# Moving the short heads' attention steps later against the projection, in a hybrid decoder layer on one core

## The chip, the core and the metric

The kernel runs on one core of one Trainium2 chip. The metric is the device time of one execution in microseconds. A core has five engines with queues of their own: TensorE (PE, matrix products), VectorE (DVE), ScalarE (ACT), GpSimd (POOL) and SyncE (SP, which issues transfers). PE writes only to PSUM, and DVE and ACT fetch its results from there.

## The reference, cut to what matters

One layer on x of 1024 positions by 2048 features, in float32:

```python
hn = rmsnorm(h, norm_mix_g)
sb_q, sb_k, sb_v, sb_g, df_q, df_k, df_v, df_g = split(hn @ w_in)
# stick-breaking heads (8 of 128): w[t,s] = beta[t,s] * prod_{s<j<t} (1 - beta[t,j]), s < t
# differential heads (8 of 2 x 64): (softmax1 - lam * softmax2) @ v, then a norm of each head's row
mixed = concat([sb_out * silu(sb_g), df_out * silu(df_g)])
h = h + mixed @ w_out
gate = sigmoid(rmsnorm(h, norm_ple_g) @ w_ple_gate)
h = h + gate * (p @ w_ple_proj)
return rmsnorm(h, norm_final_g)
```

The product of (1 - beta) over the positions between is computed as a running product along the row (a scan on VectorE).

## The kernel before, in words

**Precision.** Every large product is made of three matmuls: both operands are split into a high part in float32r and a low part (the rest), and high x high, high x low and low x high are accumulated. So each tile that becomes an operand costs a copy on ACT (high) and a subtraction on DVE (low): whi L149 and wlo L150 for weights, awh L375 and awl L376 for attention weights, v L345 and L346, q and k L1020 and L1021.

**Stages.** From 0 to about 375 us the values and gates of the short heads are projected for all positions. Then come two halves of 512 positions each, half 1 first and half 0 ("the second half") after it. In each half a loop (from L985) goes over the heads 8 to 15, the differential ones, and then 0 to 7, the stick-breaking ones ("short heads"). A differential head has two units of projection (q and k, then v and gate), a short head has one (q and k), and loads its v and gate by `load_vg` (L994). From about 1740 us the out-projection runs, then the gate, the embedding's projection and the last norm.

**Units and ticks.** `unit` (L205) makes two 128 x 512 results from 16 blocks of features: 32 times three matmuls of 512 columns (L219 to L221). After each three it calls `side.tick()`. One such step is a tick. The out-projection's first 64 products tick too (L1224 on), and what is left is run at once behind them.

**What sets the order.** `Side` (L186 to L200) keeps a queue of (due tick, step), sorted by the tick, with steps of one tick in the order in which they were added. PE's order is fixed by the order in which these steps are emitted (a manual schedule for TensorE). For ACT, DVE, POOL and SP a scheduler orders the instructions by its own reckoning; `turn` of a short head raises the priority of its splits. Each engine works its queue in order.

**The steps of a head** (`attention`, L268, returns them with due ticks counted from the end of the head's unit):
- *weights(rb, c)*, for the four row blocks of 128 queries: scores on PE (L289 to L297), mask on DVE (L302, L304), for a short head two sigmoids on ACT (pt L318, bt L319), scan (L320) and product (L321) on DVE. Differential heads: maximum, two exponentials and their combination (L325 to L336), for two components c.
- *values*: v is transposed into PSUM (vps, L343) and split into v (L345 on ACT, L346 on DVE). In half 1 it is also stored for the second half.
- *turn(pr, g)*: two row blocks form a pair pr. The pair's weights against two key blocks are transposed on PE (tp, L359) and split by `parts`: the first turn of a pair gives a triangular `lead` (L368, L369), the rest awh (L375, ACT) and awl (L376, DVE).
- *mix(pr, g)*: av += v x weights on PE (L391 with lead, L394, L395 and L396). Behind the last mix av is fetched (sm: L401 on ACT, L402 on DVE) and multiplied into sg, the head's gate (L405). With pair 1 done, `mixed` sends the result into sums in DRAM: the tensor comb_d, by a plain transfer on SP and accumulating transfers on POOL.
- *norm(pr)*, differential heads only: sums of squares on PE (L422, L423), an inverse root in `rstd_from` (L88 to L95, on ACT and DVE).

tp, vps, av and the norm's sums share two PSUM buffers (tag "t"). In half 0 a head has four turns in pair 0 and three in pair 1, and all keys; in half 1 two and one.

**The due ticks before** (L429 to L455). A short head has its row blocks at b, b + 3, b + 7 and b + 11, values at b + 14, pair 0's turns from b + 16 every 4 ticks (GAPS), pair 1's from 16 (half 0) or 12 (half 1) ticks later (SECOND), each mix one gap behind its turn; the last mix of pair 1 comes 2 later. b is 6, for head 0 it is 12. The last differential head, hd 15, is `tight`: its row blocks and turns are closer together than those of the others.

**At the end of a unit** q and k are taken from acc (qk L1018, then L1020, L1021), v and the gate are scaled (vf L1046, gf L1047), and sg is made with a sigmoid on ACT (L1050) and a product on DVE (L1055). In half 0 the other half's keys and values (k2, v2) are loaded by POOL (L1064, L1068), and the head's steps are put into the queue.

Of the kernel before, what the change touches and what calls it, by code (L numbers as in the profile page):

```python
# [14 lines left out]
F32R = mybir.dt.float32r  # L15
# [5 lines left out]
P = 128  # L21
# [12 lines left out]

GAPS, GAPD = 4, 6
SECOND = 16, 12
PRIO = 300
LATD = 11, 20
NORM_LAT = 11
# [4 lines left out]
def build(nc, tc, ap):  # L44
    with ExitStack() as ctx:
        _body(ctx, nc, tc, ap)


def _body(ctx, nc, tc, ap):
# [7 lines left out]
    V, G, A, T = nc.vector, nc.gpsimd, nc.scalar, nc.tensor  # L57
# [180 lines left out]
    v_d = dram.tile([2 * H, P, 2 * HALF], F32R, name="v_d", tag="v_d")  # L238
# [29 lines left out]
    def attention(at, pz, half, hd, q, qz, K, KL, VV, sg, vf):  # L268

        sb = hd < H  # L270
# [68 lines left out]
        def values():  # L339

            vps = pp.tile([P, 4, P], F32, name="vps", tag="t")
            for j in range(4):
                T.transpose(vps[:, j, :], vf[:, j * P:(j + 1) * P], ident)  # L343
            v = at.tile([P, 2, 4, P], F32R, name="v", tag="v")
            A.copy(v[:, 0], vps)  # L345
            V.tensor_tensor(v[:, 1], vps, v[:, 0].bitcast(F32), op=ALU.subtract)  # L346
            if half == 1:
                G.dma_start(v_d[hd], v.rearrange("p a b c -> p (a b c)"))
            VV.insert(0, v)

        def turn(pr, g):

# [8 lines left out]
            wl = at.tile([P, 2, 2 * P], F32R, name="awl", tag="awl")  # L361
            with tc.high_priority(offset=PRIO if sb else 0):
                parts(pr, g, tp, wh, wl)

        def parts(pr, g, tp, wh, wl):
            if g == 0:
                lead = at.tile([P, 2, P], F32R, name="lead", tag="lead")
                A.copy(lead[:, 0], tp[:, 0, 0:P])  # L368
                V.tensor_tensor(lead[:, 1], tp[:, 0, 0:P], lead[:, 0].bitcast(F32), op=ALU.subtract)  # L369
                wjs[pr, g] = [lead, (wh[:, 1, :], wl[:, 1, :])]  # L370
                o = slice(1, 2)
            else:
                wjs[pr, g] = [(wh[:, j, :], wl[:, j, :]) for j in range(2)]
                o = slice(0, 2)
            A.copy(wh[:, o, :], tp[:, o, :])  # L375
            V.tensor_tensor(wl[:, o, :], tp[:, o, :], wh[:, o, :].bitcast(F32), op=ALU.subtract)  # L376
# [54 lines left out]
        n1 = n0 - 1  # L431
        gap = GAPS if sb else GAPD
        if sb:
            b = 12 if hd == 0 else 6
            ss, t0 = [[b], [b + 3], [b + 7], [b + 11]], b + 16
            t1 = t0 + SECOND[half]
        else:
            tight = hd == 2 * H - 1
            s0, s1, s2, t0 = ([0, 1], [3, 5], [7, 9], 16) if tight else ([0, 2], [5, 8], [12, 15], 19)
            gap = 4 if tight else gap  # L440
            last = t0 + gap * (n0 - 1)
            s3 = [last + 1, last + (3 if tight else 5)]
            ss = [s0, s1, s2, s3]
            t1 = s3[-1] + (13 if tight else LATD[half])
        steps = [(t, partial(weights, rb, c)) for rb, ts in enumerate(ss) for c, t in enumerate(ts)]
        steps.append((t0 - 2 if sb else ss[1][-1] + 2, values))
        for pr, t, n in ((0, t0, n0), (1, t1, n1)):
            for g in range(n):
                if g:
                    steps.append((t + gap * g, partial(mix, pr, g - 1)))  # L450
                steps.append((t + gap * g, partial(turn, pr, g)))
            steps.append((t + gap * n + (2 if sb and pr else 0), partial(mix, pr, n - 1)))
            if not sb:
                steps.append((t + gap * n + (7 if tight else NORM_LAT), partial(norm, pr)))
        return steps  # L455

    with tc.tile_pool(name="at", bufs=2) as at, tc.tile_pool(name="pz", bufs=2, space=PSUM) as pz:
# [20 lines left out]
        def ftile():  # L478
            return ev.tile([P, HALF], F32, name="hc", tag="f", bufs=4)
# [256 lines left out]
        for u in range(0, H, 2):  # L736
            aa = [pp.tile([P, HALF], F32, name="pa", tag="acc", bufs=2) for _ in range(2)]
            for i in range(2):
                gv.product(u + i, 0, "A11", aa[i], True)
                s1 = ftile()  # L740
# [139 lines left out]
        for ph in range(2):  # L880
            for u in range(H):
                last = ph == 1 and u == H - 1
# [5 lines left out]
                s1 = s1s.pop(u) if early else ev.tile([P, HALF], F32, name="s1", tag="sq", bufs=2)  # L888
                if ph:
                    a = pp.tile([P, HALF], F32, name="pa", tag="acc", bufs=2)  # L890
# [6 lines left out]
                if ph == 0 and u % 3 == 2:  # L897
                    b, c = [pp.tile([P, HALF], F32, name="pb", tag="acc", bufs=2) for _ in range(2)]
                else:
                    bc = pz.tile([P, 2, HALF], F32, name="pbc", tag="z")  # L900
                    b, c = bc[:, 0, :], bc[:, 1, :]
# [66 lines left out]
        for half in (1, 0):  # L968
# [15 lines left out]
            for hd in (ORDER0, ORDER1)[half]:  # L984
                sb = hd < H  # L985
# [71 lines left out]
                VV = []  # L1057
                if half == 1:
                    G.dma_start(k_d[hd].rearrange("p (a b) -> p a b", a=2), k[:, :, 0:HALF])
                    if not sb:  # L1060
                        G.dma_start(kl_d[hd - H], KL[:, 0, :])
                else:
                    k2 = at.tile([P, 2, HALF], F32R, name="k2", tag="k2")
                    G.dma_start(k2.rearrange("p a b -> p (a b)"), k_d[hd])  # L1064
                    if not sb:
                        G.dma_start(KL[:, 1, :], kl_d[hd - H])
                    v2 = at.tile([P, 2, 4, P], F32R, name="v2", tag="v2")
                    G.dma_start(v2.rearrange("p a b c -> p (a b c)"), v_d[hd])  # L1068
                    K.append(k2)
                    VV.append(v2)  # L1070
                side.add(attention(at, pz, half, hd, q, qz, K, KL, VV, sg, vf))
                if hd >= H:
                    for kt in (2 * (hd - H), 2 * (hd - H) + 1):
# [12 lines left out]
        def pair(nm, tag, dt=F32, shape=(P, 2, HALF)):  # L1086
            return at.tile(list(shape), dt, name=nm, tag=tag, bufs=BUFS.get(tag, 2))
# [142 lines left out]
        for u in range(0, 8, 2):  # L1230
            aa = [pp.tile([P, HALF], F32, name="pa", tag="acc", bufs=2) for _ in range(2)]
            for i in range(2):
                product(u + i, 0, "A11", aa[i], True, tick=True)
                s1 = ftile()
# [66 lines left out]
        for ph in range(2):  # L1301
            for u in range(8):
                last = ph == 1 and u == 7
# [7 lines left out]
                s1 = s1s.pop(u) if early else ev.tile([P, HALF], F32, name="s1", tag="sq", bufs=2)  # L1311
                if ph:
                    a = pp.tile([P, HALF], F32, name="pa", tag="acc", bufs=2)
# [6 lines left out]
                if ph == 0 and u % 3 == 2:  # L1320
                    b, c = [pp.tile([P, HALF], F32, name="pb", tag="acc", bufs=2) for _ in range(2)]
                else:
                    bc = pz.tile([P, 2, HALF], F32, name="pbc", tag="z")
                    b, c = bc[:, 0, :], bc[:, 1, :]
# [63 lines left out]
        s2 = SumSq(ev, "ssq")  # L1388
# [54 lines left out]
        for u in range(8):  # L1443
# [9 lines left out]
            if u == 0:  # L1453
# [5 lines left out]
                s2 = SumSq(ev, "ssq")  # L1459
# [7 lines left out]
        for pc in range(4):  # L1467
            raw = wp.tile([P, 2, 2, 2, P], F32, name="wraw", tag="wraw", bufs=2)
            nc.sync.dma_start(raw, ap["w_gate"][7][pc])
            for k2 in range(2):  # L1470
# [3 lines left out]
                else:  # L1474
                    t = pair(f"wz{kk}", H1[kk], F32R, (P, 2, 2, 2, P))
# [5 lines left out]
        for tq in range(2):  # L1481
            ts = slice(tq * Q, tq * Q + Q)
            acc = [pp.tile([P, Q], F32, name=f"acq{c}", tag="acc", bufs=2) for c in range(2)]
            for c in range(2):
                for kk in range(8):
                    for kh in range(2):
                        xh, xl = X[kk + 8 * kh]
                        first = kk == 0 and kh == 0
                        last = kk == 7 and kh == 1
# [5 lines left out]
            for c in range(2):  # L1495
                t = h[0, 7 + 8 * c][:, ts]
# [73 lines left out]
```

## Time and profile before

| | us |
|---|---|
| median of 3 runs | 2514.29 (2512.94 to 2517.38) |
| the profiled execution | 2515.73 |
| its span in the trace | 2514.0 |
| PE, DVE, ACT, POOL busy | 2421.5, 1792.6, 1215.5, 279.6 |
| mean granted clock of PE | 0.991 of full speed |
| projection of short heads' v and gate | 0 to 375 |
| half 1: differential heads, short heads | 385 to 735, 735 to 1010 |
| half 0: differential heads, short heads | 1010 to 1480, 1480 to 1740 |
| out-projection and the rest | 1740 to 2514 |

Times in the profile count from the span's start. A line of a group names source line, engine, operation, output <- input, how often, then busy time, the mean duration of one, and the idle time ahead of it with its releaser. PE's matmuls are pipelined: one of 512 columns is shown as 0.39 us long, while the next starts after 0.227. So idle time between shown ends is less than what is lost against the usual distance of starts; where the text says "by starts", it counts that distance. In the timeline, [1.09 <-DVE awl L376] means that PE stood still for 1.09 us and that awl released it.

### The profile page before, as it was taken

What the parts mean: (1) busy time and instruction counts of PE and PEld (TensorE: products, weight loads), DVE (VectorE), ACT (ScalarE), POOL (GpSimd) and SP (SyncE); (2) the same over time, 40 slices, a digit from 0 to 9 for tenths busy, and PEclk for the clock granted to TensorE, in tenths of its full rate; (3) what the DMA queues carried; (4) which work ended last, traced back from release to release, by engine and by line L of the source; (5) the groups of instructions that cost most, each with busy time, mean ns of one, the idle gap of its engine ahead of it and who ended that gap; (6) DMA issues with size and microseconds to landing.
All of it is one profiled execution on the core that took longest, in us unless ns stands there. A gap on an engine that the chain in (4) does not pass through costs nothing.

```text
span 2514.0 us, 31908 instructions
## 1 busy us (share of the span) xinstructions
PE 2421.5 (96%) x11434; PEld 2005.8 (80%) x11434; DVE 1792.6 (71%) x3010; ACT 1215.5 (48%) x2067; POOL 279.6 (11%) x361
## 2 busy tenths in 40 slices
PE   8999999999999999999999988998899999999997
PEld 6787878888888887888888877887787887787886
DVE  6888777777777768688888876778577674546554
ACT  5233345555555445555566654445423224546433
POOL 1211110000000001000000000110111112330110
PEclk9999999999999999999999999999999999999998
DMA  8777654544354556343434344546746777343333
GB/s 292 255 263 223 214 193 143 164 130 151 122 153 145 168 176 186 107 113 106 122 114 122 110 122 97 143 124 186 232 162 213 169 189 230 110 137 104 131 109 101
DMA packets 167472, 397.72 MB, mean 158 GB/s; under 512 B 18897, under 2 KB 23249, under 8 KB 167313
## 3 DMA queue, kind: packets, MB, share of 16 engines
q1 hardware_dynamic: 131040, 302.07, 37.6%
q0 software_dynamic: 36272, 93.60, 14.4%
q8 instruction: 90, 1.47, 0.2%
q14 instruction: 70, 0.57, 0.1%
HBM read 297.03 MB, written 106.95 MB: 161 GB/s over the span
## 4 chain that ended last, share of the span: by engine, by line
PE 79%; DVE 10%; DMA 5%; ACT 4%; issue 3%; SPq 0%; DVEq 0%; POOL 0%; ACTq 0%
PE acc L219 16%; PE acc L220 16%; PE acc L221 16%; PE pbc L518 4%; PE pbc L516 4%; PE pbc L517 4%; PE tp L359 2%; DVE st L320 2%; PE pa L518 1%; PE pa L516 1%; PE pa L517 1%; PE av L396 1%; PE z L297 1%; PE z L298 1%; PE av L395 1%
## 5 line engine op out<-in xcount | busy, mean ns | idle before, releaser
L219 PE MATMUL acc<-xh,whi 128*128 128x512 f32 x1568 | 629.3, 401 | 1.5 <-DVE gt L1183 1.5
L221 PE MATMUL acc<-xh,wlo 128*128 128x512 f32 x1568 | 613.9, 392 | 0.0
L220 PE MATMUL acc<-xl,whi 128*128 128x512 f32 x1568 | 613.8, 391 | 0.0
L150 DVE TENSOR_TENSOR wlo<-wraw,whi 128x1024 fp32r<-128x1024 f32 x252 | 312.6, 1240 | 243.0 <-ACT whi L149 236.5
L149 ACT CAST whi<-wraw 128x1024 fp32r<-128x1024 f32 x252 | 264.9, 1051 | 295.5 <-PE acc L220 264.3
L221 PEld LDWEIGHTS acc<-xh,wlo 128*128 128x128 f32 x1568 | 295.5, 188 | 64.8
L219 PEld LDWEIGHTS acc<-xh,whi 128*128 128x128 f32 x1568 | 296.0, 189 | 57.2 <-issue 2.4
L220 PEld LDWEIGHTS acc<-xl,whi 128*128 128x128 f32 x1568 | 296.5, 189 | 54.7 <-issue 0.5
L606 ACT CAST wpr<-T 128x512 fp32r<-128x512 f32 x128 | 78.0, 621 | 317.4 <-DVE T L564 313.1
L375 ACT CAST awh<-tp 128x256 fp32r<-128x256 f32 (+1 forms) x160 | 80.1, 501 | 150.2 <-PE tp L359 124.8
L376 DVE TENSOR_TENSOR awl<-tp,awh 128x256 fp32r<-128x256 f32 (+1 forms) x160 | 92.8, 580 | 65.3 <-ACT awh L375 63.7
L328 ACT ACTIVATE et<-z,mx 128x512 f32<-128x512 f32 (+7 forms) x128 | 94.5, 738 | 51.1 <-DVE mx L325 49.5
L111 POOL TENSOR_TENSOR ssq<-ssq,sq 128x512 f32<-128x512 f32 x56 | 83.6, 1494 | 304.8 <-ACT sq L110 254.1
L320 DVE TENSOR_TENSOR_SCAN st<-pt 128x511 f32<-128x511 f32 (+3 forms) x64 | 86.5, 1352 | 23.8 <-ACT pt L318 23.8
L325 DVE TENSOR_REDUCE mx<-z 128x1 f32<-128x512 f32 (+7 forms) x128 | 96.4, 753 | 1.2
L620 DVE TENSOR_TENSOR wpr<-T,wpr 128x512 fp32r<-128x512 f32 x128 | 87.7, 685 | 5.8 <-ACT wpr L606 3.9
L396 PE MATMUL av<-awl,v 128*128 128x256 f32 x256 | 76.1, 297 | 16.0 <-DVE awl L376 15.9
L516 PE MATMUL pbc<-cS,wpr 128*128 128x512 f32 x224 | 87.4, 390 | 3.2 <-DVE u L1327 1.6
L517 PE MATMUL pbc<-cS,wpr 128*128 128x512 f32 x224 | 87.2, 389 | 0.0
L518 PE MATMUL pbc<-cS,wpr 128*128 128x512 f32 x224 | 87.2, 389 | 0.0
L318 ACT ACTIVATE pt<-z 128x512 f32<-128x512 f32 (+3 forms) x64 | 41.6, 651 | 81.6 <-DVE z L304 80.4
L394 PE MATMUL av<-awh,v 128*128 128x256 f32 x256 | 72.8, 284 | 5.5 <-ACT awh L375 5.5
(399 smaller groups left out, 5354.2 us busy)
## 6 DMA issues: line engine op xcount, KB each, us to landing
wraw<-w_in SPq DMA_DIRECT2D x192, 512.0 KB, 3.6
wraw<-w_gate SPq DMA_DIRECT2D x64, 512.0 KB, 3.6
wraw<-w_out SPq DMA_DIRECT2D x72, 256.0 KB, 3.6
wraw<-w_vg SPq DMA_DIRECT2D x71, 256.0 KB, 4.2
comb_d<-sg POOLq DMA_DIRECT2D x48, 256.0 KB, 7.5
spare<-xT SPq DMA_DIRECT2D x44, 256.0 KB, 4.2
xl<-h_d SPq DMA_DIRECT2D x40, 256.0 KB, 4.3
vghalf_d<-hc POOLq DMA_DIRECT2D x32, 256.0 KB, 4.1
```

Source lines behind the costliest of these rows:

```text
L149: A.copy(hi[:, o], raw[:, o])
L150: V.tensor_tensor(lo[:, o], raw[:, o], hi[:, o].bitcast(F32), op=ALU.subtract)
L219: T.matmul(acc[c], hi[:, k2, kh, c, :], xh, start=first, stop=False)
L220: T.matmul(acc[c], hi[:, k2, kh, c, :], xl, start=False, stop=False)
L221: T.matmul(acc[c], lo[:, k2, kh, c, :], xh, start=False, stop=last)
L320: V.tensor_tensor_scan(st[:, off + 1:nkey], pt[:, off:nkey - 1], pt[:, off:nkey - 1], initial=1.0, op0=ALU.mult, op1=ALU.bypass)
L325: V.reduce_max(mx, z[:, vw], axis=AX.X, negate=True)
L328: A.activation(et[:, vw], z[:, vw], AF.Exp, bias=mx[:, 0:1], accum_out=l)
L396: T.matmul(av, vv[:, 0, blk % 4, :], wl, start=False, stop=last)
L516: T.matmul(o, wh[:, w], xh, start=start and k == 0, stop=False, skip_group_check=True)
L517: T.matmul(o, wh[:, w], xl, start=False, stop=False, skip_group_check=True)
L518: T.matmul(o, wl[:, w], xh, start=False, stop=k == 3, skip_group_check=True)
```

## The change

- Short heads start their steps later: `LAG` gives b = 13 for all in half 1, and in half 0 b = 20 for head 0, 19 for head 1, down to 13 for head 7. So in half 0 a head's steps follow the previous head's after 31 ticks, while units follow after 32.
- In pair 1 of a short head, turns come every 5 ticks instead of 4, with each mix 5 behind its turn. The last mix comes at 15 ticks after the pair's start (14 before).
- Head 15's row blocks go from [0,1], [3,5], [7,9] to [0,2], [4,7], [10,13], its pair 0 starts at 18 (16), turns come every 5 ticks (4), the last row block at +1 and +5 (+1 and +3) behind the last turn, and pair 1 starts 14 (13) behind that.
- v2 is allocated and loaded in `values` instead of at the unit's end, and the list of v tiles is filled in order.

No computation is added or left out.

```diff
+LAG = 20, 13
...
             V.tensor_tensor(v[:, 1], vps, v[:, 0].bitcast(F32), op=ALU.subtract)
+            VV.append(v)
             if half == 1:
                 G.dma_start(v_d[hd], v.rearrange("p a b c -> p (a b c)"))
-            VV.insert(0, v)
+            else:
+                v2 = at.tile([P, 2, 4, P], F32R, name="v2", tag="v2")
+                G.dma_start(v2.rearrange("p a b c -> p (a b c)"), v_d[hd])
+                VV.append(v2)
...
         if sb:
-            b = 12 if hd == 0 else 6
+            b = LAG[half] - hd * (1 - half)
             ss, t0 = [[b], [b + 3], [b + 7], [b + 11]], b + 16
             t1 = t0 + SECOND[half]
         else:
             tight = hd == 2 * H - 1
-            s0, s1, s2, t0 = ([0, 1], [3, 5], [7, 9], 16) if tight else ([0, 2], [5, 8], [12, 15], 19)
-            gap = 4 if tight else gap
+            s0, s1, s2, t0 = ([0, 2], [4, 7], [10, 13], 18) if tight else ([0, 2], [5, 8], [12, 15], 19)
+            gap = 5 if tight else gap
             last = t0 + gap * (n0 - 1)
-            s3 = [last + 1, last + (3 if tight else 5)]
+            s3 = [last + 1, last + 5]
             ss = [s0, s1, s2, s3]
-            t1 = s3[-1] + (13 if tight else LATD[half])
+            t1 = s3[-1] + (14 if tight else LATD[half])
...
         for pr, t, n in ((0, t0, n0), (1, t1, n1)):
+            d = gap + 1 if sb and pr else gap
             for g in range(n):
                 if g:
-                    steps.append((t + gap * g, partial(mix, pr, g - 1)))
-                steps.append((t + gap * g, partial(turn, pr, g)))
-            steps.append((t + gap * n + (2 if sb and pr else 0), partial(mix, pr, n - 1)))
+                    steps.append((t + d * g, partial(mix, pr, g - 1)))
+                steps.append((t + d * g, partial(turn, pr, g)))
+            steps.append((t + d * n, partial(mix, pr, n - 1)))
             if not sb:
-                steps.append((t + gap * n + (7 if tight else NORM_LAT), partial(norm, pr)))
+                steps.append((t + d * n + (7 if tight else NORM_LAT), partial(norm, pr)))
...
-                    v2 = at.tile([P, 2, 4, P], F32R, name="v2", tag="v2")
-                    G.dma_start(v2.rearrange("p a b c -> p (a b c)"), v_d[hd])
                     K.append(k2)
-                    VV.append(v2)
```

## The prediction

> **What bounds the kernel now.** I read the page first, for which engine sets the time.
>
> ```profile
> PE 2421.5 (96%) x11434; PEld 2005.8 (80%) x11434; DVE 1792.6 (71%) x3010; ACT 1215.5 (48%) x2067; POOL 279.6 (11%) x361
> ...
> L376 DVE TENSOR_TENSOR awl<-tp,awh 128x256 fp32r<-128x256 f32 (+1 forms) x160 | 92.8, 580 | 65.3 <-ACT awh L375 63.7
> ...
> comb_d<-sg POOLq DMA_DIRECT2D x48, 256.0 KB, 7.5
> ```
>
> TensorE is busy for 96% and the change removes no instruction of it, so it can only move PE's stalls. The busy times by stretch show where those are (columns: stretch, its length, then busy time and count of PE, its weight load, DVE, ACT, POOL, then clock, DMA share, GB/s).
>
> ```profile
> 1010.00:1425.00 415.00, 415.00 (x2090) 351.41 (x2089) 332.19 (x617) 240.37 (x407) 26.29 (x37) 1.00 0.41 114
> 1425.00:1570.00 145.00, 128.76 (x647) 107.02 (x645) 105.40 (x163) 79.16 (x124) 11.24 (x15) 0.96 0.39 106
> 1570.00:1680.00 110.00, 106.16 (x567) 90.05 (x567) 84.48 (x115) 51.20 (x81) 11.25 (x15) 1.00 0.47 129
> 1680.00:1808.00 128.00, 117.68 (x608) 97.95 (x609) 90.73 (x130) 68.42 (x117) 15.54 (x21) 0.99 0.66 192
> ```
>
> From 1010 to 1425 (differential heads) PE never idles. In the second half's short heads it idles 16.2 us where head 15 hands over to heads 0 and 1, 3.8 us in three steady heads, 10.3 us in the tail that runs inside the out-projection. That is what the change can win. PE's list of waits names the releasers; first 1570 to 1680, then 1425 to 1570.
>
> ```profile
> PE av L396 <- DVE awl L376: 3.3, 3, 1.1
> PE tp L359 <- DVE sm L402: 0.7, 3, 0.2
> ```
>
> ```profile
> PE av L396 <- DVE awl L376: 4.8, 3, 2.3
> PE tp L359 <- DVE sqv L93: 3.5, 1, 3.5
> PE av L394 <- ACT awh L375: 3.3, 2, 2.0
> PE vps L343 <- DVE awl L376: 2.2, 1, 2.2
> ```
>
> So PE waits for VectorE, mostly for the low split awl of a turned tile. The timeline of one steady head shows why:
>
> ```profile
> 1603.28 2.02 DVE L320 TENSOR_TENSOR_SCAN st<-pt 128x895 f32<-128x895 f32 x1
> ...
> 1605.40 1.09 DVE L321 TENSOR_TENSOR bt<-st,bt 128x895 f32<-128x895 f32 x1
> ...
> 1605.78 0.28 PE L395 MATMUL av<-awh,v 128*128 128x256 f32 x1
> 1606.41 0.68 DVE L376 TENSOR_TENSOR awl<-tp,awh 128x512 fp32r<-128x512 f32 x1
> ...
> 1607.14 0.39 PE L396 MATMUL av<-awl,v 128*128 128x256 f32 x1 [1.09 <-DVE awl L376]
> ```
>
> awl's input was there, but DVE works in order and a scan and a product (3.1 us) stood ahead. Counted by starts, as all stalls below, L396 comes 1.36 us after L395 where such matmuls follow each other by 0.12: 1.25 lost. With 0.4 for the sm wait, 0.2 at the next mix and rounding, a steady head loses 2.05 us of its 36.7. By starts the hand-over loses 20.7 (slowed matmuls included) and the tail 13.8.
>
> **The change, part by part.** A tick is three 512-column matmuls, 3 x 0.227 = 0.68 us. The profiled run took 2515.73 (span 2514.0 and 1.73 around it), 1.4 above the median; the sum is made on it. Instruction counts stay; only places move. I use the order in which the changed program is built, with durations of rows of before: scan 2.28/2.02/1.76/1.49 (by block), product 1.23/1.09/0.96/0.82, wlo 1.23, an eviction (qk, q, k, vf, gf, v low) 0.69, lead 0.28, reduce L402 0.55, awl 0.42 or 0.69, awh 0.37 or 0.59; each DVE instruction starts about 0.09 before the last one's shown end.
>
> *Lag and five-tick turns, steady heads (1 to 4) of the second half.* Before, seven evictions of a head's unit come 26 ticks after its rb0, into the quiet pair 0. Now they come 12 to 18 ticks after it, onto rb3's scan, the values and turn (0,0), while the previous head's pair 1 still runs. Three places follow.
> (a) mix (1,0) comes 5 ticks after its turn; ahead of its awl stand wlo 1.14, mask 0.2, then rb0's scan 2.28 (after pt, 1.02), reduce 0.46, lead 0.28, product 1.14, sg 0.33, awl 0.42: 7.2 us after the last awl. PE, with turn, rb1 and 5 ticks, is there after 5.4 to 6.0: 1.5 lost (0 to 2).
> (b) The mix with the wait shown above (1,1) has five ticks instead of four, but rb1's scan, product and now wlo remain ahead: 0.5 (0 to 1.0).
> (c) Turn (0,0) and the previous head's last mix share a tick, and values come two ticks earlier. tp, vps and av take two PSUM buffers (tag t); av holds one until its last mix, so vps waits for awl (1.0; 0.4 to 2.0), and turn (0,0) now waits for v's low part, which on DVE stands behind zm, z, qk, wlo, scan and vf: 0.2 + 0.2 + 0.6 + 1.13 + 1.4 + 0.6 + 0.69 = 4.8 after that awl. PE is there after 0.5 + 1.4 + 0.7 = 2.6: 2.2 lost (1.5 to 2.8).
> Sum 5.2 against 2.05: **+12.6** for four heads (0 to +23).
>
> *A wait that is new on the path.* ScalarE's sigmoid of sg (L1050 before) waits for the comb_d transfers of the head two earlier. Before it stood behind all the splits of pair 0 but the last; now in heads 2, 3 and 4 it stands ahead of awh of mix (0,2), with the next awh and whi behind it, and PE's L394 waits for that awh. From turn (0,0) that mix is due after 12 ticks, two mixes and two turns: 10.7 us. sg's input is ready after gf, product, k, reduce, lead and L405: 2.9 us. In three steady heads of before, the last comb_d landed 10.5 to 11.4 us after L405; the page's median from issue is 7.5. With sigmoid 0.63 and awh 0.59 awh is there at 11.6 to 15.5: 0.9 to 4.8 lost. Heads' k2 and v2 loads now lie ahead of comb_d rather than beside it, so I take 9 us, 2.4 a head: **+7** (+2.5 to +14). The same wait before, where it hid nothing:
>
> ```profile
> 1510.03 0.59 ACT L375 CAST awh<-tp 128x512 fp32r<-128x512 f32 x1 [4.30 <-PE tp L359]
> 1516.03 1.28 ACT L1050 ACT_TABLE_LOAD   x1 [5.42 <-DMA comb_d<-sg]
> 1517.33 0.63 ACT L1050 ACTIVATE sg<-gf 128x512 f32<-128x512 f32 x1
> ```
>
> *Head 15 spread, head 0 at 20.* Of before's 20.7 the norm's 3.6 and head 0's last mix (4.7) shrink. The new order leaves 4.5 at head 15's mix (1,1), 1.2 at its z, 2.0 at vps and turn, 3.1 at mix (0,0), 1.9 at a turn behind L93, 4.3 at head 0's mix (1,0) behind sg's comb_d wait and table load: 17. **-3** (-12 to 0). [...]
>
> *Tail.* Heads 5 to 7 run 7 ticks later, deeper in the out-projection, whose casts and splits stand in the same queues: 4.6 at head 5's mix (1,0), 2.5 at vps, 6.4 and 3.1 at head 6's mixes, 2.4 at a turn, 1.9 at mix (0,0): 21 against 13.8: **+7** (0 to +10).
>
> *First half.* All short heads start at 13 instead of 6. Head 3's queue shows the evictions between turn (0,0) and mix (0,0), lead done about when PE comes, and k's split long before its scores (the trace has 1.29 lost there once). Before's stretch 735 to 1010 loses 13 by starts, of which 6 are in head 6's mix (0,0). **0** (-6 to +5).
>
> *v2 and its list.* On POOL the order stays k2, v2, comb_d; v2 lands in 4.5 us and is needed over 20 us later: 0.
>
> *Clock.* The granted clock after stalls:
>
> ```profile
> 1485.00:1490.00 5.00, 4.52 (x17) 3.75 (x18) 3.93 (x5) 2.80 (x4) 0.00 (x0) 0.66 0.14 55
> ...
> 1504.00:1508.00 4.00, 4.00 (x14) 3.34 (x15) 2.31 (x5) 0.59 (x1) 0.62 (x1) 0.62 0.09 35
> ...
> 1570.00:1575.00 5.00, 4.54 (x25) 3.94 (x26) 3.96 (x6) 2.94 (x4) 0.06 (x1) 1.00 0.00 0
> ```
>
> After 3.3 and 3.6 us lost PE ran slow for 1.6 and 1.1 us more; after 1.25 not at all. At 2.4 a head I add nothing; at 4.8 it would be 1.1 each. [...]
>
> Sum: 12.6 + 7 - 3 + 7 + 0 = +23.6, 2539.3 against the profiled run, **2538** beside the median.
>
> **Rivals.**
> *Faster, 2490.* DVE is busy for 84.5 of 110 us in steady heads. If scans and evictions run ahead of the places where I start the queue, the awl and v waits vanish, and the five-tick turns do what their spacing says: -8 steady, -12 hand-over, -4 tail. It decides at v's low part: done within 2.6 us after the awl before vps, nothing is lost at turn (0,0). For it: the present waits all come from crowding that this spreads. Against: in the new order the same DVE work meets in half the ticks.
> *About equal, 2515.* comb_d lands in 7.5 us (+2.5), steady heads lose only half of (c) (+6), the tail keeps its 14, the hand-over gains 9.
> *Much slower, 2560.* comb_d still takes 11.4 us: 4.8 + 1.1 in heads 1 to 5, +29 in place of 7.
> That nothing moves is excluded: the built order shows the moves.
>
> **How the numbers follow.** Forecast 0.54 (2521 to 2553), much slower 0.14, equal 0.10, faster 0.22. A measurement tells about 0.2% (5 us) from no change. Faster by more: 0.22 and a little of equal, 0.24; same 0.05; slower 0.71. The range leaves out the lower half of the faster case and part of the slowest: 2500 to 2560; the forecast's own is 2521 to 2553.
>
> **What would show it.** Right: PE waits at tp L359 (L364 in the new lines) for DVE's v, about 2 us a head; at awh behind an ACT sigmoid released by comb_d; PE idle in steady heads' 110 us near 15 to 20. Wrong: steady heads with no tp wait on v; a landing of comb_d before the ninth microsecond; a hand-over below 10 us idle; new stalls in the first half beyond 5 us.

## The result, and the profile after

The changed kernel takes 2527.74 us (median of 4, 2526.23 to 2533.56) against 2514.51 before: ratio 1.0056, 95% interval 1.0037 to 1.0074. It is slower by 13 us. The profiled execution took 2526.23, 10.5 more than the profiled one before.

The page after, first its engines, then the group and the transfer shown of before:

```profile
PE 2424.4 (96%) x11434; PEld 2008.8 (80%) x11434; DVE 1792.3 (71%) x3010; ACT 1219.1 (48%) x2067; POOL 279.7 (11%) x361
...
L381 DVE TENSOR_TENSOR awl<-tp,awh 128x256 fp32r<-128x256 f32 (+1 forms) x160 | 92.9, 581 | 71.8 <-ACT awh L380 70.2
...
comb_d<-sg POOLq DMA_DIRECT2D x48, 256.0 KB, 7.0
```

The work is the same to a few microseconds; PE's idle time moved. The same stretches as before (columns as before):

```profile
1010.00:1425.00 415.00, 415.00 (x2088) 351.39 (x2087) 332.54 (x617) 241.69 (x408) 27.19 (x38) 1.00 0.41 115
1425.00:1570.00 145.00, 133.80 (x677) 111.54 (x676) 104.02 (x164) 80.30 (x125) 11.25 (x15) 0.98 0.43 116
1570.00:1680.00 110.00, 99.03 (x521) 82.61 (x520) 77.74 (x108) 46.01 (x76) 11.25 (x15) 0.98 0.48 125
1680.00:1808.00 128.00, 109.15 (x532) 90.60 (x531) 90.30 (x125) 64.39 (x108) 11.79 (x16) 0.92 0.56 159
```

The hand-over idles 11.2 us where it idled 16.2, the steady heads 11.0 instead of 3.8, the tail 18.9 instead of 10.3. PE's waits from 1425 to 1810 (total, times, longest):

```profile
PE tp L364 <- DVE v L347: 13.5, 7, 2.9
PE av L401 <- DVE awl L381: 8.3, 11, 2.0
PE av L399 <- ACT awh L380: 7.9, 5, 2.4
PE av L396 <- DVE lead L374: 5.9, 3, 3.9
PE vps L344 <- DVE awl L381: 3.1, 4, 1.2
```

The first line did not exist before: turn (0,0) waits for the low part of v, in seven heads of eight. VectorE's timeline up to head 2's turn at 1586.06 shows what stands ahead of it:

```profile
1579.67 0.68 DVE L381 TENSOR_TENSOR awl<-tp,awh 128x512 fp32r<-128x512 f32 x1
1580.27 0.28 DVE L303 TENSOR_TENSOR zm<-z,masks 128x128 f32<-128x128 f32 x1
1580.47 0.68 DVE L1024 TENSOR_TENSOR qk<-acc,ssa 128x512 f32<-128x512 f32 x1
1581.07 0.29 DVE L305 TENSOR_TENSOR z<-z,zm 128x128 f32<-128x128 f32 x1
1581.27 1.22 DVE L151 TENSOR_TENSOR wlo<-wraw,whi 128x1024 fp32r<-128x1024 f32 x1
1582.40 0.68 DVE L1027 TENSOR_TENSOR k<-qk,k 128x512 fp32r<-128x512 f32 x1
1583.00 1.48 DVE L321 TENSOR_TENSOR_SCAN st<-pt 128x639 f32<-128x639 f32 x1
1584.71 0.69 DVE L1052 TENSOR_TENSOR vf<-vf,ssa 128x512 f32<-128x512 f32 x1 [0.23 <-DMA vf<-vg_d]
1585.32 0.68 DVE L347 TENSOR_TENSOR v<-vps,v 128x512 fp32r<-128x512 f32 x1
```

From the end of the awl that lets vps start to the end of v it takes 5.7 us, with one pause of 0.23. The values' transposes, the previous head's last mix and two ticks need about half of that.

Lost by starts, stretch by stretch (each kernel's profiled execution; the last two boundaries are 10 us later after):

| stretch (before / after) | before | after |
|---|---|---|
| 0 to 385 | 27.5 | 29.1 |
| half 1, short heads and into half 0 (735 to 1010) | 17.6 | 19.7 |
| hand-over (1430 to 1560) | 24.6 | 17.5 |
| steady heads and head 5 (1560 to 1745) | 17.0 | 33.9 |
| rest of the tail (1745 to 1790 / 1800) | 7.4 | 13.3 |
| out-projection and behind | 33.4 | 25.5 |

Up to 735 PE does the same work in the same order in both kernels, so the 1.6 us of the first row is what two executions can differ by. The last row is a gain that nobody had asked for: at 1822 and 1824 before, PE waited 2.7 and 1.1 us for split weights wpr of the out-projection, and after the change those waits are not there; the rest of the row is made of smaller waits.

These stretches are cut at fixed times, and the heads run later after the change, so head 5 falls into another row than before. Counted instead from each head's first transpose of values to the next head's, by starts:

| part of the program | before | after |
|---|---|---|
| from 1430 to head 1's values | 20.0 | 16.2 |
| heads 1 to 4 | 12.8 | 18.7 |
| heads 5 to 7, to the last mix | 15.9 | 31.6 |
| behind the last mix | 30.3 | 20.4 |

### The profile page after: what moved, and what is told of

It is laid out like the page before. It is cut to its first block, busy times and chain, and to the rows that moved or that the text cites. A ratio compares the mean times of both kernels' runs of the same rounds, so it can differ in the third digit from the quotient of the medians.

```text
span 2524.5 us, 31899 instructions
## 1 busy us (share of the span) xinstructions
PE 2424.4 (96%) x11434; PEld 2008.8 (80%) x11434; DVE 1792.3 (71%) x3010; ACT 1219.1 (48%) x2067; POOL 279.7 (11%) x361
## 4 chain that ended last, share of the span: by engine, by line
PE 75%; DVE 10%; issue 5%; DMA 5%; ACT 3%; POOL 0%; SPq 0%; DVEq 0%; ACTq 0%; POOLq 0%
PE acc L220 15%; PE acc L221 15%; PE acc L222 15%; PE pbc L524 4%; PE pbc L522 4%; PE pbc L523 4%; PE tp L364 2%; DVE st L321 2%; PE pa L524 1%; PE pa L522 1%; PE pa L523 1%; PE z L299 1%; DMA comb_d<-sg 1%; PE z L298 1%; PE av L401 1%
```

## The experiments

Each ratio is against the kernel before, run on the same chip beside it.

**One part at a time.**

*e1_lag*: gap and head 15 as before.

```diff
-            s0, s1, s2, t0 = ([0, 2], [4, 7], [10, 13], 18) if tight else ([0, 2], [5, 8], [12, 15], 19)
+            s0, s1, s2, t0 = ([0, 1], [3, 5], [7, 9], 16) if tight else ([0, 2], [5, 8], [12, 15], 19)
...
-            d = gap + 1 if sb and pr else gap
+            d = gap
...
-            steps.append((t + d * n, partial(mix, pr, n - 1)))
+            steps.append((t + d * n + (2 if sb and pr else 0), partial(mix, pr, n - 1)))
```

> Only the lag (20 to 13 in the second half, 13 in the first; v2 loaded in values); pair 1 turns every four ticks and head 15 is tight, as before. If the loss comes from the unit's evictions meeting the scans in VectorE's queue (theory), the whole loss is here: +10 to +20 us against the kernel before, with waits of tp for v's low part at turn (0,0) of 1.5 to 3 us a head. If the five-tick turns, which put the last mix into the tick of turn (0,0), are what loses (rival), this kernel is within 4 us of the kernel before.

Measured 2528.77, ratio 1.0053 (1.0037 to 1.0070). The lag alone loses as much as the whole change. tp waits for v in four heads between 1560 and 1745, 6.9 us.

*e3_nospread*: the changed kernel with the first of these edits alone (and with it the tight spacing of the last row block and pair 1).

> The changed kernel with head 15 tight as before (lag and five-tick turns stay). If spreading head 15 is what shortened the hand-over (by 7 us of stalls between 1430 and 1560), this kernel is 3 to 8 us slower than the changed one, +16 to +21 against before. If head 0's later start did it (rival), it is within 2 us of the changed kernel, +11 to +15.

Measured 2525.96, 1.0042 (1.0029 to 1.0056), which can't be told from the changed kernel. The hand-over loses 17.7 us here, 17.9 with the lag alone, 17.5 with all parts: the lag, with head 0's later start in it, shortened it, not the spread. The rival holds.

*e2_five*: the kernel before with five-tick turns only.

```diff
+            d = gap + 1 if sb and pr and hd else gap
...
-            steps.append((t + gap * n + (2 if sb and pr else 0), partial(mix, pr, n - 1)))
+            steps.append((t + d * n + (2 if sb and pr and not hd else 0), partial(mix, pr, n - 1)))
```

> The kernel before with five-tick turns in pair 1 of heads 1 to 7 alone (head 0 keeps its four ticks, since with its start at 12 its pair would run into head 1's). Evictions stay in the quiet pair 0. Theory: the wait of 1.25 us at mix (1,1) goes, and since no evictions stand in the queue, turn (0,0) waits for v less than 1 us: -6 to 0 us. Rival (the later last mix itself costs the turn): tp waits for v 1.5 to 3 us in every head, +5 to +12.

Measured 2524.32, 1.0036 (1.0022 to 1.0051). The rival holds: the 1.25 us at mix (1,1) are gone, but the last mix now comes one tick behind the next head's values, and each steady head pays two new waits, here from 1560 to 1720:

```profile
PE tp L359 <- DVE v L346: 6.5, 4, 1.6
PE vps L343 <- DVE awl L376: 3.3, 4, 0.8
```

By starts these cost 1.0 and 1.8 us a head, 2.8 in place of 2.05. The losses of lag and five ticks do not add. A likely reason, not tested by itself, is that the lag alone already puts the last mix behind the values.

*e8_half1*: only the first half's lag (`b = 13 if half else 12 if hd == 0 else 6`).

> Only the first half's lag of 13; the second half starts at 12 and 6 as before. By stretches of the two traces the first half (735 to 1010) lost 2 us more after the change than before: +1 to +4. Forecast of the prediction was 0 (-6 to +5). The rival is that the last short head of half 1, which now runs into the second half's first unit while x is loaded anew, pays 5 us there and nothing is gained before: +5 or more.

Measured 2512.00, 0.9991 (0.9982 to 1.0001): no loss. So the two microseconds in the table are not shown to be this part's price.

**Is it the PSUM chain?** awl, vps and v pass one buffer on. I broke the chain in two ways.

*e4_values0* moves values behind the last mix:

```diff
-        steps.append((t0 - 2 if sb else ss[1][-1] + 2, values))
+        steps.append((t0 if sb else ss[1][-1] + 2, values))
```

> The changed kernel with values moved two ticks later, behind the previous head's last mix in the tick of turn (0,0). The PSUM chain awl, vps, tp is broken: vps takes the buffer of the last tp, turn (0,0) takes av's. If that chain is the cause (theory), the waits of tp for v (13.5 us in 1425 to 1810) and of vps for awl (3.1) go and a wait for sm of about 1 us a head stands in their place: 6 to 11 us faster than the changed kernel, +2 to +7 against before. If the evictions crowded ahead of whatever releases the buffer are the cause (rival), tp waits for sm about as long as it did for v, since in the built order sm's reduction also stands behind qk, wlo, scan and vf: within 4 us of the changed kernel.

Measured 2537.19, 1.0096 (1.0082 to 1.0109): 10 us slower than the changed kernel, which is outside both expectations. The wait for v is gone, and a longer one has its place (1425 to 1810):

```profile
PE tp L364 <- DVE sm L407: 24.5, 8, 5.2
```

*e7_v2* moves the last mix two ticks ahead instead (`t + d * n - (2 if sb and pr else 0)`).

> The changed kernel with the last mix of pair 1 two ticks earlier, in the tick of the next head's values and ahead of them; values stay where they are. Like the kernel with later values it breaks the PSUM chain, but sm's reduction has two ticks (1.4 us) more before turn (0,0). Theory: tp waits for sm under 1 us, 8 to 12 us faster than the changed kernel, +1 to +5 against before. Rival (crowded evictions): tp waits about 1 us, 3 to 6 faster than the changed kernel.

Measured 2532.43, 1.0079 (1.0066 to 1.0093): about 5 us slower than the changed kernel, again outside both expectations. tp waits 10.4 us for sm, and the wait for awl at av rises from 8.3 to 13.1.

*e5_five_last* is e2_five with the last mix four ticks behind the last turn, where it was before the change:

```diff
-            steps.append((t + d * n + (2 if sb and pr and not hd else 0), partial(mix, pr, n - 1)))
+            steps.append((t + d * n + (0 if not (sb and pr) else -1 if hd else 2), partial(mix, pr, n - 1)))
```

> The kernel before with five-tick turns in pair 1 of heads 1 to 7, as in the run with five ticks alone, but with the last mix four ticks behind the last turn: at 14 ticks as before, in the tick of the next head's values and ahead of them. If the order of last mix and values decides (theory), the waits of 1.0 (vps) and 1.8 us (tp for v) a head go and the 1.25 at mix (1,1) stays away: -8 to -3 us against before. If the five ticks themselves cost (rival), +5 or more.

Measured 2518.60, 1.0024 (1.0014 to 1.0034): 6 us worse than before, as the rival had it. The median ratio is below e2_five's, but the two intervals overlap. A steady head now loses 0.8 at mix (0,3) and 0.8 at its last mix for awl, and 0.9 at tp for sm: the same sum at other places.

So the theory of the chain fell: in three tries another instruction freed the buffer, and none of the three kernels was clearly faster than the one it varies. The trace of e4_values0 shows why for head 2: sm's reduction at 1589.12 stands behind qk, wlo, k, the same scan and vf on VectorE, much as v's low part did. That this row of work is the cause was tested only further down, by e8_rb3.

**The wait for comb_d.** *e6_gate* takes the changed kernel and makes the sigmoid of sg a step of its own, issued behind the last awh:

```diff
+                def gate(sg=sg, gf=gf):
+                    with tc.issue_after(lastawh[0].ins):
+                        lastsig[0] = A.activation(sg, gf, AF.Sigmoid)
+                    V.tensor_tensor(sg, sg, gf, op=ALU.mult)
...
+                if late:
+                    side.add([(14 - hd, gate)])
```

> The changed kernel with the sigmoid of sg of short heads 1 to 7 of the second half issued behind the awh that mix (0,2) needs, not ahead of it. The prediction priced the wait for comb_d ahead of that awh at 7 us: then this kernel is 5 to 9 us faster than the changed one. By the trace ACT does wait 2.4 to 4.0 us for comb_d there, but PE lost only 1.0, 0 and 1.8 us at mix (0,2) of heads 2 to 4 (theory now): 1 to 4 us faster.

Measured 2515.62, 1.0014 (1.0005 to 1.0022): about 0.4%, 10 us, better than the changed kernel, more than the trace had let me expect. The larger part is not at mix (0,2). In the changed kernel ACT, at the hand-over, stood still for 6.2 us:

```profile
1524.42 1.28 ACT L1056 ACT_TABLE_LOAD   x1 [6.20 <-DMA comb_d<-sg]
1525.72 0.64 ACT L1056 ACTIVATE sg<-gf 128x512 f32<-128x512 f32 x1
1527.32 1.02 ACT L319 ACTIVATE pt<-z 128x1024 f32<-128x1024 f32 x1 [0.97 <-DVE z L305]
1528.24 1.02 ACT L320 ACTIVATE bt<-z 128x1024 f32<-128x1024 f32 x1
1529.14 0.27 ACT L406 COPY sm<-av 128x128 f32<-128x128 f32 x1
1529.29 0.30 ACT L373 CAST lead<-tp 128x128 fp32r<-128x128 f32 x1
```

and lead, which head 0's mix (1,0) needs, came after all of this; PE lost 4.1 us there and 2 more to awl and a slow clock (granted 0.50 from 1531.3 to 1535.3). In e6_gate that mix loses nothing, and the hand-over loses 11.7 us instead of 17.5. The waits for v stay (13.9 us).

*e9_bgate* is the same edit on the kernel before (gate step at tick 9).

> The kernel before with only the sigmoid of sg of short heads 1 to 7 of the second half issued later, behind the awh of the last turn of pair 0. Before, ACT idles 5.4 us for comb_d ahead of that sigmoid at 1516, and head 0's last mix loses 4.7 us and 1 us of slow clock to it. Theory (the comb_d wait on ACT is a loss of its own, whatever the lag): -7 to -4 us against before. Rival (another wait takes its place, awl behind VectorE's scans): within 2 us.

Measured 2509.24, 0.9984 (0.9974 to 0.9994): 4 to 5 us faster, the size that the theory had. The hand-over gains 9.4 us by starts (24.6 to 15.2) and the steady stretch gives 7.3 back (17.0 to 24.3), where mix (1,1) now waits 1.6 to 2.3 for awl. So the rival's wait is there too, but takes back only a part. By the code the later sigmoid also holds gf's buffer longer, and the next gate's load then lands too late for its place on VectorE. gf's group on VectorE, 1560 to 1720 (busy, mean ns, idle time before):

```profile
L1047 DVE TENSOR_TENSOR gf<-gf,ssa 128x512 f32<-128x512 f32 x4 | 2.8, 692 | 9.8 <-DMA gf<-vg_d 9.8
```

The kernel before shows no such wait in that stretch.

**The scans.** *e8_rb3* is e6_gate with row block 3 six ticks later in the second half:

```diff
-            ss, t0 = [[b], [b + 3], [b + 7], [b + 11]], b + 16
+            ss, t0 = [[b], [b + 3], [b + 7], [b + (17 if half == 0 else 11)]], b + 16
```

> The kernel with sg's sigmoid behind awh (run e6_gate), and in the second half row block 3 of each short head six ticks later (17 instead of 11 behind row block 0; it is first needed by pair 1). Its scan (1.5 us) then no longer stands ahead of v's low part, which by the built order has qk, wlo and k ahead of it: 3.0 us after the awl instead of 4.8, where PE comes after 2.6. If turn (0,0) waits for whatever VectorE has queued ahead of the release (theory), tp's waits for v (13.9 us in 1425 to 1810) fall below 5 and the kernel is 6 to 11 us faster than e6_gate: -9 to -3 us against before, faster than both kernels. If the evictions alone are enough to hold v (rival), the waits stay above 10 us and the time within 3 us of e6_gate.

Measured 2504.37, 0.9958 (0.9945 to 0.9970): 10 us faster than before, faster than both kernels. Its waits from 1425 to 1810:

```profile
PE vps L344 <- DVE awl L381: 10.0, 8, 2.6
PE av L401 <- DVE awl L381: 8.6, 13, 1.7
...
PE tp L364 <- DVE v L347: 0.5, 3, 0.2
```

One scan of 1.5 us (and its share of sigmoids on ACT), which nobody needs for another 16 ticks, was what held v back: 13.9 fell to 0.5. vps, which waits for an awl behind row block 2's scan, rose from 3.7 to 10.0, so the two waits together fell from 17.6 to 10.5.

That does not make the late heads better than before the change. Counted by heads as above, heads 1 to 4 lose 13.5 us (12.8 before) and heads 5 to 7 lose 21.9 (15.9). The gain over the kernel before lies ahead of head 1's values, 8.9 against 20.0, and behind the last mix, 22.2 against 30.3.

*e10_rb23* moves row block 2 as well (17 and 21).

> The kernel of run e8_rb3 with row block 2 of the second half's short heads ten ticks later as well (row blocks 2 and 3 at 17 and 21 behind row block 0; both are first needed by pair 1 at 32). In e8_rb3 tp's wait for v is gone and 10.0 us of PE's idle time is vps waiting for an awl that stands behind row block 2's scan and product (2.5 us). If scans ahead of a PSUM release are the loss (theory), that wait falls below 4 us, the scans fall between the turns of pair 0, and the kernel is 4 to 8 us faster than e8_rb3: -18 to -14 us against before. If the scans only move their delay to the awl of pair 0's turns (rival), the time is within 3 us of e8_rb3.

Measured 2505.83, 0.9962 (0.9948 to 0.9976), no better than e8_rb3: the rival holds. vps waits 1.0 us, but the scans now stand ahead of awl in pair 0:

```profile
PE av L401 <- DVE awl L381: 11.2, 15, 1.9
PE av L399 <- ACT awh L380: 6.7, 4, 3.0
PE msq L427 <- DVE awl L381: 3.2, 1, 3.2
```

*e11_before_rb23*: the same row blocks on e9_bgate, without the lag.

> The kernel of run e9_bgate (before, with sg's sigmoid behind awh) with row blocks 2 and 3 of the second half's short heads at 17 and 21 behind row block 0. It asks whether the lag is of any use once scans and sigmoid are out of the way. The scans leave mix (1,1), where the steady heads of before lose 1.25 us (1.6 to 2.3 in e9_bgate): -6 to -14 us against before by theory, short of e10_rb23 by 3 to 8 us, since head 15's hand-over keeps its norm wait of 3.6 us. Rival: the moved scans meet the unit's evictions (which come at 26) and the gain is gone: within 3 us of e9_bgate.

Measured 2523.28, 1.0043 (1.0027 to 1.0058). The expectation failed on its sign. In each steady head mix (1,1) loses 1.1 to 1.7 us for awh and 2.3 for awl. Here is VectorE ahead of head 2's:

```profile
1594.81 0.69 DVE L1047 TENSOR_TENSOR gf<-gf,ssa 128x512 f32<-128x512 f32 x1 [2.69 <-DMA gf<-vg_d]
...
1598.05 2.29 DVE L320 TENSOR_TENSOR_SCAN st<-pt 128x1023 f32<-128x1023 f32 x1 [0.23 <-ACT pt L318]
1600.44 1.22 DVE L321 TENSOR_TENSOR bt<-st,bt 128x1023 f32<-128x1023 f32 x1
...
1602.92 2.01 DVE L320 TENSOR_TENSOR_SCAN st<-pt 128x895 f32<-128x895 f32 x1
1605.04 1.09 DVE L321 TENSOR_TENSOR bt<-st,bt 128x895 f32<-128x895 f32 x1
1606.05 0.68 DVE L376 TENSOR_TENSOR awl<-tp,awh 128x512 fp32r<-128x512 f32 x1
```

Row block 3's scan and product (1585.56 to 1587.97) now come between two evictions and push them back; VectorE then stands for gf, and row blocks 0 and 1 come so late that both their scans stand ahead of awl. How much of this is the scans and how much the held gate buffer was not taken apart, so what the lag alone is worth once the scans are moved stays open; the two kernels with lag, scans moved and late sigmoid are the fastest here.

## Why the prediction was right or wrong

The direction and the mechanism were right: the recorded 2538 is 10 us above the result, and the result lies in the recorded range and inside the forecast's own, 2521 to 2553. The size was off by more than a factor of two on the profiled executions, 23.6 against 10.5. That the total came no further off is in part luck, because misses of both signs met. Counted by heads, heads 1 to 4 were put at +19.6 (12.6 and 7) and lost 5.9 more than before; heads 5 to 7 were put at +7 and lost 15.7 more; what lies behind the last mix was put at nothing and lost 9.9 less. Of the signs named ahead, the wait of tp for v came; PE's idle time in the 110 us was 11.0, short of the 15 to 20. Step by step, by starts:

- **(c), turn (0,0) behind v: right.** Forecast 1.0 and 2.2 a head. Heads 2, 3 and 4 lost 0.8 and 3.1, 0.4 and 2.3, 1.3 and 1.9: 3.3 on the mean. Head 1, for which the same was forecast, lost 0 and 1.2, which makes 2.75 over the four. The buffer was named, and what stood ahead of v. That the buffer as such is not the cause, only e4 and e7 showed.
- **(a), mix (1,0): wrong.** Forecast 1.5; measured 0.5 or less. I let DVE start its list at the last awl of mix (0,3). In head 2 it did the wlo and the mask at 1600.83 and 1602.71, and PE's mix at 1608.91 lost nothing; a wait of PE elsewhere gives it more time; the sum treats each wait as if nothing had been caught up.
- **(b), mix (1,1)**: 0.5 forecast, 0.7 at most: right.
- **The sigmoid ahead of awh: right in mechanism, mis-sized and misplaced.** Forecast 2.4 at each mix (0,2) of heads 2 to 4; measured 1.0, 0 and 1.8, though ACT stood 4.0, 2.4 and 3.5 us for comb_d. In these heads comb_d let the sigmoid go 7.7 to 7.9 us after L410, where I had taken 9; a landing before the ninth microsecond had been named as a sign of being wrong. With 7.8 the sum would have had 1.2 a head. What this wait costs is mostly in the hand-over, which the forecast had as 4.3 at head 0's mix (1,0): 4.1 and 0.9 were lost. In e6_gate, where the sigmoid stands behind the awh that PE needs, the kernel is 10 us faster.
- **Hand-over: -3 forecast, -3.8 measured up to head 1's values: right in size.** (The table's fixed stretch has -7.1, since before the change it reaches further into head 1.) The items were less good. Of them z (1.2 and 0.95), vps and turn (2.0 and 2.05) and head 0's mix hold; head 15's mix (1,1) was put at 4.5 and lost 0.6. That the spread of head 15 does it was no claim of the sum, and e3 shows that it does not.
- **Tail, heads 5 to 7: +7 forecast, +15.7 measured: wrong in size.** (The stretch from 1745 shows only 5.9 of it, since head 5's waits fall into the one ahead.) Two large items hold: head 5's mix (1,0), 4.6 forecast and 4.1 lost, and one of head 6's mixes, 6.4 and 6.2 (mix (0,0)). Head 5's turn (0,0) and mix (0,2), 2.9 and 3.5, were not in the sum. Nor was the clock, which the prediction put at nothing: from 1680 to 1808 the granted clock is 0.92, where it was 0.99. Matmuls with no wait ahead of them lost 10.8 us in these heads, 4.2 before, most of it in the slow stretches behind the waits.
- **Left out:** the out-projection behind the tail, -7.9 (-9.9 behind the last mix). I summed to the last late head and not to the next wait of the same engines, so a wait that goes there could not appear. This, (a) and the tail with its clock are the terms that failed. Why the weights were ready in time was not tried.
- **First half: 0 forecast, and e8_half1 measured 0.9982 to 1.0001.** In the changed kernel 3.1 us are lost at 959.90 where acc waits for qk L1024 beside the reload of x, and other waits there went.
- **The rivals.** The faster case was said to decide at v's low part, done within 2.6 us after the awl. It came after 5.7 at head 2, where 4.8 was forecast: k stood ahead as well, and vf waited for its load. e8_rb3 then came near that condition by taking the scan out (2.9 us at head 2, with a wait of 0.2 left), and was 10 us faster than before. The equal case had comb_d right (7.5 assumed, 7.7 to 7.9 seen), but its tail did not stay at 14. For the much slower case comb_d would have had to take 11.4.

## What to carry to other kernels

When a step is moved on a kernel whose bound engine waits for an in-order helper, list what stands in the helper's queue between the input and the release that the bound engine needs; here the name of the buffer mattered less than that list, and three tries with another release from the same queue won nothing. Look first for work in that list that is not needed yet, and try moving that; then look where it goes, since in e10_rb23 and e11_before_rb23 the moved scans stood ahead of other releases. A wait for a transfer on a helper's queue is to be placed behind, not ahead of, the work that the bound engine needs next, and its price must be looked for at every place that the queue feeds.

## What the runs showed of the hardware

In these traces PE's clock does not follow the length of a wait alone. After 2.13 us of idle time at 1564.38 in e9_bgate it ran at about half speed for some 3.2 us (first line, 0.57 over 4 us); after 2.89 us at 1586.06 in the changed kernel it did not slow at all (second line, 1.00); after 3.94 us at 1531.37 it did (third line, 0.50). The granted clock is the third number from the end.

```profile
1564.30:1568.30 4.00, 3.92 (x14) 3.55 (x15) 2.96 (x5) 3.06 (x4) 0.00 (x0) 0.57 0.00 0
```

```profile
1586.00:1590.00 4.00, 3.94 (x22) 3.42 (x23) 2.76 (x7) 0.64 (x2) 1.57 (x3) 1.00 0.66 185
1531.30:1535.30 4.00, 3.36 (x12) 2.87 (x13) 4.00 (x7) 3.27 (x5) 0.00 (x0) 0.50 0.00 0
```
